# Activation slots of 8704 instead of 8320 bytes in a two-layer encoder trunk on one core

## Chip, cores and metric

The kernel runs on one core of one Trainium2 chip. The metric is the device time in microseconds of one execution. "Faster", "same" and "slower" refer to the median of the kernel before, 1147.99 us.

## What is computed

Two layers of an encoder trunk for 256 tokens of 1024 channels, float32. Each has a token mixer of three branches and a squared-ReLU MLP, both between norms that a vector c modulates:

```
h = rms_norm(x, g_pre_mix) * (1.0 + sc_m) + sh_m
proj = h @ w_in                                  # 1024 x 12296, all branches and gates
y_ret = silu(rg) * head_norm(retention(rope(rq), rope(rk), rv))
y_lru = gelu(ly) * rg_lru(causal_conv(lx, ...), ...)
y_fox = forgetting_attention(fq, fk, fv, log_sigmoid(ff + b_f))
merged = g0 * (y_ret @ ret_w_o) + g1 * (y_lru @ lru_w_o) + g2 * (y_fox @ fox_w_o)
x = x + gt_m * rms_norm(merged @ w_out, g_post_mix)
h = rms_norm(x, g_pre_mlp) * (1.0 + sc_f) + sh_f
x = x + gt_f * rms_norm(square(relu(h @ w1)) @ w2, g_post_mlp)
```

The shift, scale and gate vectors (sh, sc, gt) come from silu(c) @ ada_w + ada_b.

## The kernel before

**Products in three parts.** Every float32 operand x of a product is split into a high part xh (x rounded to the type fp32r) and a low part xl = x - xh. A product is the sum of three matmuls, xh with wh, xl with wh and xh with wl; the helper mm3 (lines 343, 344 and 345) issues the three, and all large products go through it. So a matmul reads one operand that is loaded into TensorE (an instruction of its own, on the row PEld of the profile) and one that streams through it. In the profile's rows a matmul is written out<-streamed,loaded.

**Tiling.** Weights come in chunks, each in two halves of 512 KB (128 partitions x 1024 floats). In `gemm` a weight chunk is loaded 128 columns at a time and the activations stream, 256 tokens wide: 8 k-steps x 2 column blocks x 3 = 48 matmuls of 256 columns. In `gemm_n` it is the other way round (the fv columns). In `gemm_wide` (the weights rv of layer 1, w_o, the first quarter of w1, and w2) activations are loaded and weights stream 512 columns wide. In `first_rows`, at the start of layer 0, rv and rq/rk are computed while the adaLN rows of the first norm are still being summed.

**Order and staging.** One list, ORDER, fixes the order of all weight chunks, adaLN chunks among them. A chunk's halves arrive by DMA from the SyncE queue in a ring of five raw tiles (wraw). ScalarE copies a half to the high part (whi, line 219) and VectorE subtracts (wlo, line 220); both go into rings of four slots. `prefetch` keeps two or three chunks split ahead. An adaLN chunk is not split, VectorE sums it (line 275). Smaller work (heads of retention, the gates of the recurrence, the heads of attention) is cut into steps that are put between the chunks by a budget.

**The activation slots.** The pool `up` holds, behind a first tile of 64 bytes ("phase"), twelve slots of one size: T6, T7, hh, hl, T1, T2, T3, T4, T5, T8, T9 and T10, in the order of their first use. `U(tag, ...)` returns a view of a slot; with other=True it starts 64 bytes (PHASE = 16 floats) into the slot. What lies in them: hh and hl are the high and low part of the normed input; T1 and T2 hold rq (both parts in T1), rk (T2, other=True), yr (high in T1, low in T2), fq, mh/ml and the MLP's hidden mih/mil in turn; T3 and T4 rv, yl, fv and mih/mil; T5 and T6 fk (other=True); T7 and T8 yf. Some weight chunks are split into free activation slots (wown, always with other=True; both parts of a half in one slot, 4096 bytes apart).

The pools in order are cpool (constants, pth and ptl, the modulation), wp (five wraw, four whi, four wlo, 4224 bytes each), up, tp (temporaries of 2048 bytes, uh and ul among them) and sp (small columns). A tile's place within 512 bytes follows from the sizes of what stands before it. Where `up` begins, its first slot, T6, is called place 320 in this text; wp's slots then stand at 0, 128, 256 and 384, and pth and ptl at 384.

The functions that the change touches:

Of the kernel before, what the change touches and what calls it, by code (L numbers as in the profile page):

```python
# [15 lines left out]
PSUM = bass.MemoryType.PSUM  # L16
KH = 4
PHASE = 16
NRAW = 5
NHL = 4  # L20
PL = None
# [11 lines left out]
P = 128  # L33
D = 1024
# [83 lines left out]
def trunk_kernel(ctx, tc, x, c, vec, con, ffw, wts, out):  # L118
# [4 lines left out]
    up = ctx.enter_context(tc.tile_pool(name="up", bufs=1))  # L123
# [7 lines left out]
    V, A, T = nc.vector, nc.scalar, nc.tensor  # L131
    up.tile([P, PHASE], F32, name="phase")

# [67 lines left out]
    def raw_half(i, extra=None):  # L201
        n = C if extra is None else C + NH_F
        t = wp.tile([P, KH, n], F32, name="wraw", tag="wraw", bufs=NRAW)
        src = wts[pos[0], i]
# [27 lines left out]
    def split_of(l, name, cix):  # L232
        parts = []
        for i in range(2):
            t = early.pop(0) if early else raw_half(i, ffw[l] if (name, cix) == ('fv', 0) else None)
            n = t.shape[-1]
            if (name, cix) in SLOTS:
                own = SLOTS[name, cix][i]
            elif name in ('w1', 'w2') and (name, cix) < ('w2', 12):
                own = SPARE_SLOTS[spare[0] % len(SPARE_SLOTS)]  # L240
                spare[0] += 1
            else:
                own = PL
            if own:
                both = U(own, [P, 2, KH, C], F32R, "wown", True)
                hi, lo = both[:, 0], both[:, 1]
            else:
                hi, lo = split_tiles(n)
            split(t, hi, lo)
            parts.append((hi, lo))  # L250
        pos[0] += 1
        if wide(name, cix):
            parts = [[p.rearrange("p (k j) c -> p k (j c)", k=2) for p in hl] for hl in parts]
            return [(parts[k // 2][0][:, k % 2, :], parts[k // 2][1][:, k % 2, :]) for k in range(KH)]
        return [(parts[k // KH][0][:, k % KH, :], parts[k // KH][1][:, k % KH, :]) for k in range(KD)]
# [146 lines left out]
    def U(tag, shape, dt, name, other=False):  # L402

        o, n = PHASE * other, math.prod(shape[1:])
        t = up.tile([P, 2 * D + 2 * PHASE], dt, name=name, tag=tag)[:, o:o + n]
        dims = {c: k for c, k in zip("abc", shape[1:])}
        return t.rearrange(f"p ({' '.join(dims)}) -> p {' '.join(dims)}", **dims)

# [8 lines left out]
    def new_h():  # L417
        return (U("hh", [P, KD, S], F32R, "hh"), U("hl", [P, KD, S], F32R, "hl"))
# [13 lines left out]
    def first_rows():  # L432


        silu_rows()
        xn = U("T6", [P, 2, D], F32, "xn")
        xr = U("T7", [P, KD, S], F32, "xr")

# [753 lines left out]
```

## Time and profile before

| | us |
|---|---|
| median of 3 runs | 1147.99 (1147.07 to 1148.08) |
| the profiled execution | 1149.36 |
| its span, first to last instruction | 1147.6 |
| TensorE matmul busy | 1122.1 |
| TensorE weight load busy | 1055.2 |
| VectorE busy | 872.4 |
| ScalarE busy | 616.6 |
| GpSimd busy | 33.2 |

The granted TensorE clock is 0.997 on average. The DMA moved 255 MB. A busy time is the time that is covered by an engine's records. [...] In the rows of groups the number after x is the count, then come busy us and the mean ns of one record, and behind the second bar the engine's idle time before them.

### The profile page before, as it was taken

What the parts mean: (1) busy time and instruction counts of PE and PEld (TensorE: products, weight loads), DVE (VectorE), ACT (ScalarE), POOL (GpSimd) and SP (SyncE); (2) the same over time, 40 slices, a digit from 0 to 9 for tenths busy, and PEclk for the clock granted to TensorE, in tenths of its full rate; (3) what the DMA queues carried; (4) which work ended last, traced back from release to release, by engine and by line L of the source; (5) the groups of instructions that cost most, each with busy time, mean ns of one, the idle gap of its engine ahead of it and who ended that gap; (6) DMA issues with size and microseconds to landing.
All of it is one profiled execution on the core that took longest, in us unless ns stands there. A gap on an engine that the chain in (4) does not pass through costs nothing.

```text
span 1147.6 us, 20486 instructions
## 1 busy us (share of the span) xinstructions
PE 1122.1 (98%) x8164; PEld 1055.2 (92%) x8164; DVE 872.4 (76%) x1323; ACT 616.6 (54%) x912; POOL 33.2 (3%) x54
## 2 busy tenths in 40 slices
PE   6999999999899999999999999999999999999997
PEld 5999999999899889989879999999999997989986
DVE  6898788878797789888586768877878778956543
ACT  6676594544455555444455658655444655644441
POOL 0001000000000100000020010000000001000000
PEclk9999999999999999999999999999999999999999
DMA  9954546579776569888745454565777574875541
GB/s 357 401 173 159 185 135 211 182 247 318 271 256 220 201 215 319 317 308 311 255 149 180 149 186 164 166 202 186 234 267 258 188 266 147 291 240 187 189 151 63
DMA packets 74284, 255.43 MB, mean 223 GB/s; under 512 B 10108, under 2 KB 12492, under 8 KB 74188
## 3 DMA queue, kind: packets, MB, share of 16 engines
q1 hardware_dynamic: 74188, 254.12, 65.4%
q8 instruction: 64, 1.05, 0.4%
q14 instruction: 32, 0.26, 0.1%
HBM read 253.00 MB, written 1.09 MB: 221 GB/s over the span
## 4 chain that ended last, share of the span: by engine, by line
PE 83%; DMA 6%; DVE 5%; issue 4%; ACT 1%; POOL 1%; DVEq 0%; POOLq 0%; SPq 0%; ACTq 0%
PE ps L345 24%; PE ps L343 24%; PE ps L344 24%; DMA wraw<-in_wts_dram 5%; DVE wlo L220 2%; DVE wraw L275 1%; PE xT L427 1%; PE rvp L344 1%; PE rvp L345 1%; PE rvp L343 1%; PE qkp L344 1%; PE qkp L345 1%; PE qkp L343 1%; POOL rs_v L188 1%; ACT whi L219 0%
## 5 line engine op out<-in xcount | busy, mean ns | idle before, releaser
L219 ACT CAST whi<-wraw 128x1024 fp32r<-128x1024 f32 (+1 forms) x286 | 299.2, 1050 | 282.6 <-PE ps L344 164.5
L220 DVE TENSOR_TENSOR wlo<-wraw,whi 128x1024 fp32r<-128x1024 f32 (+1 forms) x286 | 348.4, 1223 | 101.7 <-ACT whi L219 101.3
L343 PE MATMUL ps<-hh,whi 128*128 128x256 f32 x1312 | 369.5, 282 | 2.8 <-DVE fkl L650 1.2
L345 PE MATMUL ps<-hh,wlo 128*128 128x256 f32 x1312 | 368.7, 281 | 0.0
L344 PE MATMUL ps<-hl,whi 128*128 128x256 f32 x1312 | 368.3, 281 | 0.0
L343 PEld LDWEIGHTS ps<-hh,whi 128*128 128x128 f32 x1312 | 246.3, 188 | 4.3 <-PE ps L345 2.0
L345 PEld LDWEIGHTS ps<-hh,wlo 128*128 128x128 f32 x1312 | 247.7, 189 | 0.0
L344 PEld LDWEIGHTS ps<-hl,whi 128*128 128x128 f32 x1312 | 247.1, 188 | 0.2
L275 DVE SCALAR_TENSOR_TENSOR wraw<-wraw,sir 128x1024 f32<-128x1024 f32 x82 | 100.2, 1223 | 41.4 <-DMA wraw<-in_wts_dram 41.0
L220 DVE TENSOR_TENSOR wown<-wraw,wown 128x1024 fp32r<-128x1024 f32 x72 | 87.2, 1222 | 26.5 <-ACT wown L219 26.5
L219 ACT CAST wown<-wraw 128x1024 fp32r<-128x1024 f32 x72 | 74.8, 1048 | 51.8 <-PE ps L345 27.2
L345 PE MATMUL ps<-whi,mil 128*128 128x512 f32 x144 | 56.9, 395 | 0.0
L344 PE MATMUL ps<-wlo,mih 128*128 128x512 f32 x144 | 56.8, 394 | 0.0
L343 PE MATMUL ps<-whi,mih 128*128 128x512 f32 x144 | 56.7, 394 | 0.0
L344 PE MATMUL ps<-wlo,hh 128*128 128x256 f32 (+1 forms) x144 | 45.8, 318 | 0.0
L343 PE MATMUL ps<-whi,hh 128*128 128x256 f32 (+1 forms) x144 | 45.7, 317 | 0.0
L345 PE MATMUL ps<-whi,hl 128*128 128x256 f32 (+1 forms) x144 | 45.6, 317 | 0.0
L344 PE MATMUL ps<-hl,wown 128*128 128x256 f32 x160 | 45.0, 281 | 0.0
L345 PE MATMUL ps<-hh,wown 128*128 128x256 f32 x160 | 44.9, 281 | 0.0
L343 PE MATMUL ps<-hh,wown 128*128 128x256 f32 x160 | 44.8, 280 | 0.0
L343 PE MATMUL ps<-wown,mih 128*128 128x512 f32 x112 | 44.2, 395 | 0.0
L345 PE MATMUL ps<-wown,mil 128*128 128x512 f32 x112 | 44.1, 394 | 0.0
(336 smaller groups left out, 2290.2 us busy)
## 6 DMA issues: line engine op xcount, KB each, us to landing
wraw<-in_wts_dram SPq DMA_DIRECT2D x440, 512.0 KB, 4.2
wfirst<-in_wts_dram SPq DMA_DIRECT2D x28, 512.0 KB, 10.2
rows<-drow SPq DMA_DIRECT2D x10, 512.0 KB, 5.1
xs<-in_x_dram SPq DMA_DIRECT2D x2, 512.0 KB
out_dram<-xs SPq DMA_DIRECT2D x4, 256.0 KB, 2.0
csb<-in_con_dram SPq DMA_DIRECT2D x1, 768.0 KB
csb<-in_con_dram SPq DMA_DIRECT2D x1, 256.0 KB, 9.5
vsb<-in_vec_dram SPq DMA_DIRECT2D x1, 152.0 KB
```

The costliest lines, as they stand in the source:

```text
L188: eng.tensor_scalar(v, total, scale, EPS, ALU.mult, ALU.add)
L219: A.copy(hi, t)
L220: V.tensor_tensor(lo, t, hi.bitcast(F32), ALU.subtract)
L275: V.scalar_tensor_tensor(t, t, 0.5, sir, ALU.mult, ALU.mult, accum_out=m)
L343: T.matmul(ps, ah, bh, start=start, stop=False, **kw)
L344: T.matmul(ps, ah, bl, start=False, stop=False, **kw)
L345: T.matmul(ps, al, bh, start=False, stop=stop, **kw)
L427: i = T.transpose(pt[:, k, :], x[:, (k0 + k) * P:(k0 + k + 1) * P], ident)
```

## The change

The length of a slot goes from 2 x 1024 + 2 x 16 = 2080 floats (8320 bytes) to 2 x 1024 + 128 = 2176 floats (8704 bytes). Views into a slot start where they did, at its beginning or 64 bytes on. 8320 is 16 x 512 + 128, 8704 is 17 x 512. Nothing else is touched.

```
 PHASE = 16
+SLOT_PAD = 128
 NRAW = 5
...
     def U(tag, shape, dt, name, other=False):

         o, n = PHASE * other, math.prod(shape[1:])
-        t = up.tile([P, 2 * D + 2 * PHASE], dt, name=name, tag=tag)[:, o:o + n]
+        t = up.tile([P, 2 * D + SLOT_PAD], dt, name=name, tag=tag)[:, o:o + n]
         dims = {c: k for c, k in zip("abc", shape[1:])}
```

More of the change, by code (lines that the diff above doesn't have):

```diff
@@ L18 @@
 PHASE = 16
+SLOT_PAD = 128
 NRAW = 5
@@ L404, in U @@
         o, n = PHASE * other, math.prod(shape[1:])
-        t = up.tile([P, 2 * D + 2 * PHASE], dt, name=name, tag=tag)[:, o:o + n]
+        t = up.tile([P, 2 * D + SLOT_PAD], dt, name=name, tag=tag)[:, o:o + n]
         dims = {c: k for c, k in zip("abc", shape[1:])}
```

## The prediction

> **What bounds the kernel now.** I read the page first, for the shares and the chain, then TensorE's groups kept apart by shape, then the granted clock and counts in stretches, and last the timeline of single matmuls.
>
> ```profile
> span 1147.6 us, 20486 instructions
> PE 1122.1 (98%) x8164; PEld 1055.2 (92%) x8164; DVE 872.4 (76%) x1323; ACT 616.6 (54%) x912; POOL 33.2 (3%) x54
> ...
> GB/s 357 401 173 159 185 135 211 182 247 318 271 256 220 201 215 319 317 308 311 255 149 180 149 186 164 166 202 186 234 267 258 188 266 147 291 240 187 189 151 63
> ...
> PE 83%; DMA 6%; DVE 5%; issue 4%; ACT 1%; POOL 1%; DVEq 0%; POOLq 0%; SPq 0%; ACTq 0%
> ```
>
> TensorE is busy for 98% of the span and holds 83% of the chain that ended last. So the time is the number of matmuls times the step from one to the next, and the question is whether the change moves that step. A busy time is no step, because the records overlap; the step comes from counts in a stretch, or from starts in the timeline.
>
> ```profile
> core 0: us, PE busy (x), PEclk, DMA share, GB/s
> 353.00:373.00 20.00, 20.00 (x179) 1.00 0.80 263
> 724.00:809.00 85.00, 85.00 (x724) 1.00 0.58 186
> 242.00:315.00 73.00, 69.06 (x575) 1.00 0.86 294
> 816.00:878.00 62.00, 61.00 (x514) 1.00 0.78 262
> 408.00:578.00 170.00, 170.00 (x1030) 1.00 0.84 290
> 560.00:577.00 17.00, 17.00 (x75) 1.00 0.72 248
> ```
>
> The first two stretches hold matmuls of 256 columns alone, and TensorE never idles in them. A record of 0.28 us lies across each border, so about 2.4 are counted too many. 724 to 809: 85,000 / (724 - 2.4) = 117.8 ns a step. 353 to 373: 20,000 / (179 - 2.4) = 113.3 ns. Same shape, same line of code, same clock (1.00), and the faster stretch has the busier DMA (0.80 against 0.58), so neither the clock nor traffic makes the difference.
>
> What differs is which tiles are read:
>
> ```profile
> L343 PE MATMUL ps<-hh,whi 128*128 128x256 f32 x1312 | 369.5, 282 | 2.8 <-DVE fkl L650 1.2 <-DVE fvl L650 0.8 <-DVE fql L886 0.7
> L345 PE MATMUL ps<-hh,wlo 128*128 128x256 f32 x1312 | 368.7, 281 | 0.0
> L344 PE MATMUL ps<-hl,whi 128*128 128x256 f32 x1312 | 368.3, 281 | 0.0
> L344 PE MATMUL ps<-hl,wown 128*128 128x256 f32 x160 | 45.0, 281 | 0.0
> L345 PE MATMUL ps<-yrh,wlo 128*128 128x256 f32 x128 | 36.0, 281 | 0.0
> L345 PE MATMUL ps<-ylh,wlo 128*128 128x256 f32 x128 | 36.0, 281 | 0.0
> L345 PE MATMUL ps<-yfh,wlo 128*128 128x256 f32 x128 | 35.4, 276 | 0.0
> L344 PE MATMUL ps<-yfl,whi 128*128 128x256 f32 x128 | 35.4, 276 | 0.0
> ```
>
> After "<-" stands first the operand that streams, then the one that was loaded. Only the pair yfh, yfl shows 276 ns; hh/hl, yrh/yrl and ylh/yll show 280 to 282. Stretch 353 to 373 is the w_f stage, with yfh and yfl. Adding up the slots in the order in which they are first used (T6, T7, hh, hl, T1, T2, T3, T4, T5, T8, T9, T10; a slot is 8320 bytes, 16 x 512 + 128), and calling the place of T6 within 512 bytes 320, I get T7 448, hh 64, hl 192, T1 320, T2 448, T3 64, T4 192, T5 320, T8 448, T9 64, T10 192. The pairs hh/hl, yr (T1, T2) and yl (T3, T4) each lie 128 bytes apart; yf (T7, T8) is the one pair that starts at one place, and the one that is fast.
>
> **What a single stretch shows.** Rows of the timeline (start, duration, line, tiles):
>
> ```profile
> 143.71 0.28 PE L344 MATMUL lg<-ul,wown 128*128 128x256 f32 x1
> 144.95 0.28 PE L343 MATMUL ps<-hh,whi 128*128 128x256 f32 x1
> 145.06 0.28 PE L344 MATMUL ps<-hl,whi 128*128 128x256 f32 x1
> 145.42 0.28 PE L344 MATMUL ps<-hl,whi 128*128 128x256 f32 x1
> ```
>
> ```profile
> 622.96 0.28 PE L343 MATMUL rs<-rq,rk 128*128 128x256 f32 x1
> 623.30 0.28 PE L343 MATMUL ps<-hh,whi 128*128 128x256 f32 x1
> 623.89 0.28 PE L345 MATMUL ps<-hh,wlo 128*128 128x256 f32 x1
> ```
>
> uh and ul start at one place (slots of 2048 bytes, 4 x 512, in the pool behind T10, so at 192 + 128 = 320), and so do the halves of rq (T1, 320). The first burst takes 1.24 us for 11 steps, 113 ns each; as soon as hh and hl alternate, three steps take 0.36 us, 120 each. The second: three steps in 0.34 us (113), then five in 0.59 us (118). So a stream at one place can run at 113, and the jump by 128 bytes between hh and hl ends it. But equal places do not suffice:
>
> ```profile
> 136.51 0.28 PE L343 MATMUL lg<-uh,wown 128*128 128x256 f32 x1
> 137.93 0.28 PE L343 MATMUL ps<-hh,whi 128*128 128x256 f32 x1
> ...
> 80.69 0.28 PE L343 MATMUL rs<-rq,rk 128*128 128x256 f32 x1
> 81.75 0.28 PE L343 MATMUL ps<-hh,whi 128*128 128x256 f32 x1
> ...
> 351.26 0.28 PE L344 MATMUL fo<-ptl,fvh 128*128 128x256 f32 x1
> 352.57 0.28 PE L343 MATMUL ps<-yfh,whi 128*128 128x256 f32 x1
> 352.91 0.28 PE L343 MATMUL ps<-yfh,whi 128*128 128x256 f32 x1
> ```
>
> Another burst of the same kinds keeps the slow step: lg 1.42 us for 12 (118), rs 1.06 us for 9 (118), fo 1.31 us for 11 (119; pth and ptl, too, share a place). There are two paces, and a stream at one place keeps the one it fell into for a dozen matmuls. Behind the slow fo, yf was at 113 at once (0.34 us for three) and stayed there, while its weights rotated through four slots of 4224 bytes, 8 x 512 + 128, so 128 apart.
>
> **The change part by part.** The program does not change: the same instructions, queues and waits. Only addresses move. A slot of 8704 bytes is 17 x 512, so all twelve begin at 320 (those taken with other=True at 384, as T1, T5 and T6 do now). The pools behind move by 12 x 384 = 4608 = 9 x 512 bytes and keep their places; wp and cpool, in front, do not move.
>
> (1) Matmuls of 256 columns whose streamed pair comes to one place. hh/hl: 1312 x 3 from the rows, 480 with weights in own slots (160 x 3) and 192 for rq and rk in first_rows (8 x 8 x 3 by its loops): 4608. yr and yl: 128 x 3 each, 768. Together 5376, each worth up to 117.8 - 113.3 = 4.5 ns, or 24.2 us. But the gain counts only where TensorE sets the pace. In the stretches 242 to 315 and 816 to 878 it idles 3.9 and 1.0 us, and what is late there is the weights:
>
> ```profile
> 250.92 4.82 DMA wraw<-in_wts_dram
> 255.80 1.11 issue
> ...
> L344 PE MATMUL ps<-hl,whi 128*128 128x256 f32 x112 | 31.5, 281 | 0.0
> ```
>
> The first two are rows of the chain: a load of 4.8 us and its consumer's turn, one such pair behind the other. The last one is the group of hl and whi in the stretch 242 to 315, and 816 to 878 has the same: 112 x 3 x 2 = 672 of the 5376 lie there, and faster ones would only wait longer. I take nothing for them (between 0 and 672 x 4.5 = 3.0 us). That leaves 4704 x 4.5 = 21.2 us. How many get the fast pace? At worst none (the slow lg, rs and fo), at best all (yf). The streams concerned are long, 48 matmuls and more in a row, which is nearer to yf than to bursts of 12; but each is broken by small bursts that stream from 384, and after such a break it must find the fast pace again. I take 85%: 18 us.
>
> (2) Matmuls of 512 columns:
>
> ```profile
> L343 PE MATMUL ps<-whi,mih 128*128 128x512 f32 x144 | 56.7, 394 | 0.0
> L343 PE MATMUL ps<-wown,mih 128*128 128x512 f32 x112 | 44.2, 395 | 0.0
> ```
>
> (144 + 112) x 3 = 768 with mih/mil, and 96 for each of six quads (4 chunks x 4 k x 2 halves x 3: w_o and the first w1 in both layers, rv once by first_quad and once in first_rows), 1344 in all. They stream weights whose two halves share a place already; it is the loaded hh/hl, mh/ml or mih/mil that come together. Stretch 560 to 577: 17,000 / (75 - 1.7) = 231.9 ns; twice 113.3 is 226.6. So between nothing and 1344 x 5.3 = 7.1 us. No row shows such a stream with both pairs together, and streamed pairs that agree do not give it the fast pace now: I take nothing.
>
> (3) Supply. In 408 to 578 the DMA moves 290 GB/s while TensorE never idles; its 1030 matmuls in 170 us make some 600 of 256 columns and 430 of 512, so the gain there is 600 x 4.5 = 2.7 us, 1.6%, and asks for 295 GB/s. Slices of 28.7 us on the page reached 308 to 319, so I take no loss; were the supply at its end, the 2.7 us would be lost.
>
> (4) VectorE and ScalarE read the moved slots too:
>
> ```profile
> L220 DVE TENSOR_TENSOR wlo<-wraw,whi 128x1024 fp32r<-128x1024 f32 (+1 forms) x286 | 348.4, 1223 | 101.7 <-ACT whi L219 101.3
> L220 DVE TENSOR_TENSOR wown<-wraw,wown 128x1024 fp32r<-128x1024 f32 x72 | 87.2, 1222 | 26.5 <-ACT wown L219 26.5
> ```
>
> 1223 ns in the pool of weights, 1222 in the slots: nothing.
>
> Sum: -18 us. The profiled execution took 1149.36 us around its span of 1147.6, 1.37 above the median of the runs, 1147.99; I take the difference to the median: 1130 us, a gain of 1.6%.
>
> [...]
>
> **The rivals.** *Nothing happens* (1146 to 1150). Addresses are not the cause, or the common place 320 leaves the streams at the slow pace. For it: lg, rs and fo at 118 to 119 with equal places, two of them at 320; yf, the one long fast stream, stands at 448. Against it: lg and rs at 320 also ran at 113, and yf reached 113 straight from a slow burst. Then 0 x 4.5, 1148 us. The slow pace at 320 has 10 in 100, addresses that never matter 2. [...]
>
> *Only part of it* (1139 to 1146). Each break throws the stream back, and it recovers late: 20 to 40% of 21.2 us, 4 to 8 us, about 1142. 12 in 100.
>
> *Slower.* The common place is on the wrong side of the two paces: at 448 yf always fell into the fast one, at 320 streams keep the slow. Then yf, 384 matmuls, loses 4.5 ns each, 1.7 us, and if the slow pace of a stream at one place is that of fo, 119 instead of 117.8, 5376 x 1.2 = 6.5 us come on top: 8 us, 1156. It decides once fewer than 30% find the fast pace (0.3 x 21.2 against 0.7 x 6.5 + 1.7). 9 in 100.
>
> **How the numbers follow.** The forecast, fast pace for most, has 67 in 100, with its own range from 1121 (all 4704, 21, and some 6 of parts 1 and 2 left at nothing) to 1139 (40% of 21). The whole range is 1121 to 1149, which takes in the two milder rivals and leaves out about 9 above and 6 below. About 0.2%, 2.3 us, is what a measurement of this kernel can tell from no change. Faster: the forecast and the part, 0.79. Same: 0.12. Slower: 0.09.
>
> **What would show it.** In the groups by shape, hh/hl, yr and yl at 276 to 277 ns instead of 281, yf unchanged; in the long stretches a step of 113 to 114 ns; the order of work unchanged; more idle time of TensorE, with the same loads of weights late, around 242 to 315. Wrong: yf at 281, or hh/hl still at 281 while the time falls; wrong in size, if the 512-column groups (394 ns now) move as well.

## The result and the profile after

The changed kernel takes 1133.23 us (median, 1132.45 to 1133.79); the kernel before, beside it, 1148.03. The ratio is 0.9872, with a 95% interval from 0.9855 to 0.9889: 14.8 us or 1.3% faster. The prediction had 1130 us, 18 us faster.

The profiled execution's span fell from 1147.6 to 1132.0 us. From the page after (first lines and the head of the chain):

```profile
span 1132.0 us, 20486 instructions
PE 1103.7 (98%) x8164; PEld 1038.6 (92%) x8164; DVE 872.0 (77%) x1323; ACT 616.8 (54%) x912; POOL 33.9 (3%) x54
...
PE 85%; DMA 5%; DVE 4%; issue 3%; ACT 1%; POOL 1%; DVEq 0%; POOLq 0%; SPq 0%; ACTq 0%
```

The counts are the same, VectorE and ScalarE are as busy as before, and TensorE alone is 18.4 us less busy. TensorE's groups by shape, after:

```profile
L344 PE MATMUL ps<-hh,whi 128*128 128x256 f32 x1312 | 366.0, 279 | 5.1 <-DVE fql L887 3.0 <-DVE fvl L651 1.4 <-DVE fkl L651 0.6
L346 PE MATMUL ps<-hh,wlo 128*128 128x256 f32 x1312 | 364.4, 278 | 0.1
L345 PE MATMUL ps<-hl,whi 128*128 128x256 f32 x1312 | 364.3, 278 | 0.0
L345 PE MATMUL ps<-hl,wown 128*128 128x256 f32 x160 | 44.3, 277 | 0.0
L346 PE MATMUL ps<-yrh,wlo 128*128 128x256 f32 x128 | 35.4, 276 | 0.0
L346 PE MATMUL ps<-ylh,wlo 128*128 128x256 f32 x128 | 35.4, 276 | 0.0
L346 PE MATMUL ps<-yfh,wlo 128*128 128x256 f32 x128 | 35.4, 277 | 0.0
```

yr and yl fell from 281 to 276 ns, as yf had been. hh and hl stand at 278 and 279, between the two paces. The idle time before the first group rose from 2.8 to 5.1 us.

The stretch from w_r to the end of w_l in layer 0, after (busy, count, clock, DMA share, GB/s):

```profile
165.00:239.00 74.00, 74.00 (x655) 1.00 0.63 202
```

74,000 / (655 - 2.4) = 113.4 ns a step. In the timeline, a stream of hh and hl after ropv:

```profile
89.28 0.28 PE L344 MATMUL ps<-hh,whi 128*128 128x256 f32 x1
...
92.10 0.28 PE L344 MATMUL ps<-hh,whi 128*128 128x256 f32 x1
...
92.57 0.28 PE L345 MATMUL ps<-hl,whi 128*128 128x256 f32 x1
...
93.48 0.28 PE L344 MATMUL ps<-hh,whi 128*128 128x256 f32 x1
```

The first 24 steps take 2.82 us (117.5 each). At 92.10 the chunk's second half begins, which lies in another weight slot; from 92.57 on eight steps take 0.91 us (114). The next stream does not get free:

```profile
95.85 0.28 PE L345 MATMUL ps<-hl,whi 128*128 128x256 f32 x1
...
101.39 0.28 PE L344 MATMUL rs<-rq,rk 128*128 128x256 f32 x1
```

47 steps in 5.54 us, 118 each, through the change of slots as well. So both paces go on side by side. From here on "the fast share" is the share of steps of at most 115 ns between the starts of hh/hl matmuls of 256 columns, counted over the whole trace (pauses over 150 ns left out). It rose from 10% to 67%, and the mean step fell from 117.76 to 114.85 ns. For yr and yl all steps are fast (113.3); yf, fast before, went from 113.4 to 113.9 ns.

The 117.8 of before and the slow 117.8 of after look alike only in the mean. Before, with the pair apart, the steps of hh and hl vary, mostly between 115 and 122 ns, and only 2% of them are at 114 or less; the 10% are mostly single steps of 115. After, a slow stream steps evenly, mostly at 117 to 119 ns, and 65% of all steps are at 114 or less.

Counted over all streams, pauses left out, no stream after the change switches pace within a weight slot, apart from the first five steps of a stream or a slot. At a change of slots all of the more than 100 streams at 113 ns stay there. Those at 118 ns come to 113 in 29 of 43 cases where the streamed tile lay 64 bytes behind the loaded one (mod 256: both places taken within 256 bytes) and then lies 192 behind, and in none of the 3 the other way round.

Last, what became of the lead. The first matmul of fv and the first of the attention heads, before:

```profile
244.09 0.29 PE L343 MATMUL pf<-whi,hh 128*128 128x264 f32 x1
...
297.52 0.28 PE L922 MATMUL fs<-ch,sel 128*128 128x256 f32 x1
```

and after:

```profile
239.04 0.29 PE L344 MATMUL pf<-whi,hh 128*128 128x264 f32 x1
...
293.42 0.28 PE L923 MATMUL fs<-ch,sel 128*128 128x256 f32 x1
```

A lead of 5.05 us at the one is 4.10 at the other: between them the weights' DMA sets the pace (the chain after is loads of 4.6 to 5.7 us, one behind the other, and TensorE idles 2.4 of 54.4 us), and 0.95 us of what TensorE saved is spent waiting. Layer 1 gives back 1.1 us there (13.3 and 12.2).

### The profile page after: what moved, and what is told of

It is laid out like the page before. It is cut to its first block, busy times and chain, and to the rows that moved or that the text cites. A ratio compares the mean times of both kernels' runs of the same rounds, so it can differ in the third digit from the quotient of the medians.

```text
span 1132.0 us, 20486 instructions
## 1 busy us (share of the span) xinstructions
PE 1103.7 (98%) x8164; PEld 1038.6 (92%) x8164; DVE 872.0 (77%) x1323; ACT 616.8 (54%) x912; POOL 33.9 (3%) x54
## 4 chain that ended last, share of the span: by engine, by line
PE 85%; DMA 5%; DVE 4%; issue 3%; ACT 1%; POOL 1%; DVEq 0%; POOLq 0%; SPq 0%; ACTq 0%
PE ps L346 25%; PE ps L344 25%; PE ps L345 25%; DMA wraw<-in_wts_dram 5%; DVE wlo L221 2%; PE xT L428 1%; DVE wraw L276 1%; PE rvp L345 1%; PE rvp L346 1%; PE rvp L344 1%; PE qkp L344 1%; PE qkp L345 1%; PE qkp L346 1%; POOL rs_v L189 1%; ACT whi L220 0%
## 5 line engine op out<-in xcount | busy, mean ns | idle before, releaser
L346 PE MATMUL ps<-hh,wlo 128*128 128x256 f32 x1312 | 364.4, 278 | 0.1
L345 PE MATMUL ps<-hl,whi 128*128 128x256 f32 x1312 | 364.3, 278 | 0.0
```

The lines of the kernel that those rows point to most:

```text
L345: T.matmul(ps, ah, bl, start=False, stop=False, **kw)
L346: T.matmul(ps, al, bh, start=False, stop=stop, **kw)
```

## The experiments

The theory: a matmul's step depends on where in 256 or 512 bytes its two streams begin; a jump between the high and low part of the streamed operand throws it to the slow pace. The first rival: it is the slots' length or their common place that counts, not the pair.

**e1_low128: the pairs apart again, in the long slots.**

```
-        o, n = PHASE * other, math.prod(shape[1:])
+        o, n = PHASE * other + 32 * (tag in ('hl', 'T2', 'T4', 'T8')), math.prod(shape[1:])
```

> Slots of 8704 bytes as in the change, but what lies in hl, T2, T4 and T8 (the low parts) begins 128 bytes further on, so every high and low part is 128 bytes apart again. If the distance within a streamed pair sets the step, hh/hl, yr, yl and now yf too run at 280 to 282 ns a record, a step of 117.5 to 118, and the time is 1147 to 1150 us. If it is the length of the slots, or the place of the high parts, the time stays at 1133 us.

1149.07 us, ratio 1.0004 (0.9994 to 1.0015): the whole gain is gone. (Two small changes cancel in this: yf at 117.8 instead of 113.4 ns costs 1.7 us against the kernel before, and the 512-column matmuls at 230.5 instead of 231.6 save 1.5.) Groups of this kernel:

```profile
L345 PE MATMUL ps<-hl,whi 128*128 128x256 f32 x1312 | 368.1, 281 | 0.0
L346 PE MATMUL ps<-yrh,wlo 128*128 128x256 f32 x128 | 36.0, 281 | 0.0
L346 PE MATMUL ps<-yfh,wlo 128*128 128x256 f32 x128 | 35.9, 281 | 0.0
```

yf, fast in both kernels, is slow here. The length of the slots is ruled out.

**e2_low256: 256 bytes apart.** The same line with 64 floats instead of 32.

> As e1_low128, but the low parts begin 256 bytes further on. If what repeats in the memory repeats every 256 bytes, 256 apart is as good as nothing apart and the time is 1133 us within 4; if it repeats every 512, it is 1147 to 1150 us.

1131.47 us, ratio 0.9852 (0.9828 to 0.9875), fast share 65%: as the change. So 256 bytes apart did as well as one place, where 128 apart lost the whole gain (1149.07 us in e1_low128); "the same place within 512" asks for more than these runs needed.

**e11_low64: 64 bytes apart.** The same line with 16 floats.

> e1_low128 with 64 instead of 128 bytes between high and low part. If any distance that is no multiple of 256 throws a stream back, hh/hl, yr and yl run at 117 to 118 a step and the time is 1146 to 1150 us; if small distances do less, between 1136 and 1145.

1152.96 us, ratio 1.0048 (1.0033 to 1.0063), fast share 14% (single steps of 115 ns; 1% are at 114 or less), mean step of hh/hl 118.7 ns. That is slower than the kernel before, which I had not expected. 64 bytes on, the low part lies 128 behind half of the weight slots and level with the other half; in this trace hh/hl, yr, yl and yf step at 117.7 ns on the first half and at 119.5 on the second. Level was worse than apart in e8_rel0 too (120.2 ns, below).

**e4_hh_only: one pair alone.** The kernel before, with one slot longer:

```
-        t = up.tile([P, 2 * D + 2 * PHASE], dt, name=name, tag=tag)[:, o:o + n]
+        t = up.tile([P, 2 * D + 2 * PHASE + 96 * (tag == 'hh')], dt, name=name, tag=tag)[:, o:o + n]
```

> The kernel before, with the slot of hh alone 384 bytes longer: hh and hl begin at one place, and yr, yl and also T7 and T8 (yf) lie 128 apart. If the pair decides, hh/hl fall to 277 to 279 ns as in the change, yr and yl stay at 281 and yf rises from 276 to 281; gain about 13 us at hh/hl less 1.7 at yf, 1136 to 1139 us. If it is the common length of all slots, yf stays at 276 and the time at 1148 us.

1138.93 us, ratio 0.9915 (0.9895 to 0.9935). Its groups:

```profile
L344 PE MATMUL ps<-hl,whi 128*128 128x256 f32 x1312 | 364.5, 278 | 0.0
L345 PE MATMUL ps<-yrh,wlo 128*128 128x256 f32 x128 | 36.0, 281 | 0.0
L344 PE MATMUL ps<-yfl,whi 128*128 128x256 f32 x128 | 35.9, 281 | 0.0
```

Each pair by itself: hh/hl fast as in the change, yr still slow, yf now slow. Here the profile of one kernel holds the effect in both directions.

**e3_at448: the common place moved by 128 bytes.**

```
-    up.tile([P, PHASE], F32, name="phase")
+    up.tile([P, PHASE + 32], F32, name="phase")
```

> The change, with the first tile of the pool 192 instead of 64 bytes long, so that all slots (and the pools behind) begin at 448 instead of 320. In the profile after the change a stream that is slow never turned fast inside a weight slot, only where the weights change slots, and only from a slot that lies 64 bytes before the activations (mod 256) to one that lies 192 before; every chunk begins at 64. If only the distance within the pair matters, 1133 us within 2, with about two thirds of the hh/hl matmuls at 113. If the place against the weights decides how a stream begins, chunks now begin at 192: more than 85% at 113, and 1126 to 1129 us.

1131.28 us, ratio 0.9853 (0.9827 to 0.9879); fast share 77%, less than the 85% expected, and the ratio's interval overlaps that of the change. Of the 13 streams that follow a float32 product or transpose and begin at the chunks' usual place, 12 now begin fast; in the change 1 of 13 does. Streams at 118 ns now come to 113 where 64 becomes 192 from slot to slot, which lies at the chunks' borders here. I took this for proof that the place against the weights decides how a stream begins, and built on it.

**e5_rel192, e6_rel64, e8_rel0: the weights at one place.** All ring slots of whi and wlo begin at one place (mod 256), so a stream sees no jump between ring slots. The three differ in the pool's first tile alone (48, 16 and 64 floats).

```
-        return (wp.tile([P, KH, n], F32R, name="whi", tag="whi", bufs=NHL),
-                wp.tile([P, KH, n], F32R, name="wlo", tag="wlo", bufs=NHL))
+        return [wp.tile([P, 1088], F32R, name=tag, tag=tag, bufs=NHL)[:, :KH * n].rearrange("p (k c) -> p k c", k=KH)
+                for tag in ("whi", "wlo")]
...
-SLOT_PAD = 128
+SLOT_PAD = 64
```

> Slots of 8448 bytes (33 x 256), whi and wlo slots of 4352 (17 x 256), and the pool 128 bytes further on: now every streamed activation lies 192 bytes behind every loaded weight (mod 256), through all slots. Theory: the place of streamed against loaded decides how a stream begins after a break; at 192 nearly all begin fast and none is thrown back, so 85 to 97% of the hh/hl matmuls at 113 and 1125 to 1129 us; only the streams behind ropv and fo (pth stays where it is) begin slow and, without a change of place to free them, stay slow. Rival: only the jump of the weight slots frees a stream, and without it less than 60% are fast, 1135 us or more.

1140.88 us, ratio 0.9934 (0.9912 to 0.9957), fast share 32%: the theory of the beginning fell, its rival came true.

> As e5_rel192, but the pool stays where it was, so that every streamed activation lies 64 bytes behind every weight of the rings (192 behind those in own slots). Theory: at 64 streams begin slow and never turn; fast only what comes in from an already fast stream (those behind lg or w1's own-slot weights): 20 to 45% of hh/hl fast, 1136 to 1143 us. Rival, only the distance within the pair counts: as the change, 1131 to 1134 us.

1143.03 us, ratio 0.996 (0.9944 to 0.9976), fast share 24%. As expected in size, but it is hardly worse than 192 and so does not speak for the reason given.

> As e5_rel192, but activations and ring weights begin at one and the same place (0 behind; 192 behind the own-slot weights). If only the distance within the streamed pair counts, 1131 to 1134 us. If the place against the weights counts, this is the meeting of both streams at one place and should be the worst: hardly any of the hh/hl with ring weights at 113, 1140 us or more.

1156.0 us, ratio 1.0081 (1.0058 to 1.0104), slower than the kernel before. The stretch of w_r to w_l, in this kernel:

```profile
170.00:240.00 70.00, 70.00 (x585) 1.00 0.60 192
```

70,000 / (585 - 2.4) = 120.2 ns: with both streams beginning at one place even a pair without a jump ran slower here than the slow pace of 117.8. These are activations that stream past ring weights. For the 512-column matmuls of the same kernel, where weights stream past loaded activations, one place cost nothing: 228.4 ns a step there, 230.2 where the weights lie 64 behind.

**e7_all_pairs: every stream at one place against every weight.** e5_rel192 with fq, fv and rv at other=True, fk without it, and pth/ptl 64 bytes further on.

> e5_rel192 with the rest brought to the same two places: fq, fv and rv (loaded) begin 64 bytes into their slots, fk (streamed) at the slot's beginning, pth and ptl (streamed) 64 bytes further on. So everything that streams 256 columns of activations lies at 192 behind everything that is loaded. Theory: no break is left, over 97% of all 256-column matmuls fast, 1122 to 1126 us. Rival: breaks come from switching between kinds of matmul and not from places, then it is as e5_rel192 within 1 us.

1138.77 us, ratio 0.993 (0.9906 to 0.9953), fast share 42%: the theory's 97% and 1126 us did not come. The rival was nearer: the time is 2.1 us below that of e5_rel192, and the intervals overlap. The shortest account of what goes on is in two stretches of this one kernel, the same code at the same places in layer 0 and in layer 1:

```profile
165.00:240.00 75.00, 75.00 (x665) 1.00 0.61 198
721.00:799.00 78.00, 78.00 (x665) 1.00 0.56 184
```

75,000 / 662.6 = 113.2 ns and 78,000 / 662.6 = 117.7. In layer 1 a stream had fallen into the slow pace earlier, and it stayed in it from the start of w_r to the end of w_l. Nothing is to be seen that would free it: no slot begins elsewhere, and TensorE never pauses. Over the whole traces it is the same: of streams that had been slow for more than eight matmuls, none turned fast at a change of weight slots that brought no jump, 0 of 122 in e5_rel192, 0 of 106 in e6_rel64 and 0 of 95 here. So it is at the jumps of the weight slots, to which the theory had given no part, that slow streams came free (29 of 43 in the profile after the change), and there the jumps hurt none of the more than 100 fast ones. (Not every jump does it: the only five from 64 to 192 that met a slow stream in e6_rel64, from a ring slot into an activation slot, freed none.)

**e9_jumps and e10_jumps448: more such jumps.** Ring slots begin at one place, but within them each k-step lies 128 bytes further on:

```
-    def split_tiles(n):
+    def split_tiles(n, jump=False):
+        w = 288 if jump else n
+        return [wp.tile([P, 1152], F32R, name=tag, tag=tag, bufs=NHL)[:, :KH * w].rearrange(
+            "p (k c) -> p k c", k=KH)[:, :, :n] for tag in ("whi", "wlo")]
...
-                hi, lo = split_tiles(n)
+                hi, lo = split_tiles(n, n == C and not wide(name, cix))
```

with SLOT_PAD = 64; e10_jumps448 also has the pool's first tile at 48 floats.

> The runs at fixed places showed slow streams that stayed slow for 100 us and more: nothing frees a stream but a jump of the loaded weights. Here the ring slots of the weights are 4608 bytes and begin at one place, but inside a slot each k-step lies 128 bytes further on (rows of 288 instead of 256 floats; chunks read 512 wide stay as they were); activation slots of 8448, pool where the change has it (64 behind the weights at the first k-step, then 192, 64, 192). So the jump from 64 to 192 comes twice in a slot instead of once in two. Theory: a slow stream is freed after some 12 to 24 matmuls, 75 to 90% of hh/hl fast, 1127 to 1131 us. Rival, the place at which a stream begins decides alone: as the change or slower, 1133 us or more.

1130.36 us, ratio 0.985 (0.9834 to 0.9867), fast share 86%, as the theory had it. Of the streams that had been slow for more than eight matmuls, 18 of 18 turned fast at a jump from 64 to 192 and 0 of 16 at one from 192 to 64. The time alone would not tell this version from the change (after_again, below, on the same chip: 0.9848 to 0.9883). By the steps, hh/hl save 3.9 us more than in the change (114.0 against 114.85 ns), and the 512-column matmuls cost 1.7 us more (231.4 against 230.1 ns).

> e9_jumps with the pool 128 bytes further on: streams begin 192 behind the weights, and the weights that stream 512 wide lie 64 behind the loaded activations, the pairing that took 229 ns a step instead of 232 in the change. Theory: 80 to 95% of hh/hl fast and all 512-column matmuls at about 229: 1124 to 1129 us. Rival as before: e3_at448's 1131 us or more.

1127.47 us, ratio 0.9826 (0.9811 to 0.984), fast share 92%. Its groups and the stretch of w_r to w_l:

```profile
L346 PE MATMUL ps<-hl,whi 128*128 128x256 f32 x1312 | 362.6, 276 | 0.0
L345 PE MATMUL ps<-whi,mih 128*128 128x512 f32 x144 | 56.1, 389 | 0.0
```

```profile
162.00:236.00 74.00, 74.00 (x655) 1.00 0.62 197
```

hh and hl are at 276 now, and the 512-column group, 394 in the kernel before and 393 in the change, is at 389 (a mean step of 228.9 ns). The stretch steps at 74,000 / 652.6 = 113.4 ns, as in the change, where it was fast already. This version beats both kernels, as expected.

**after_again: the change once more,** on the chip of the last three and beside them.

> The change itself, on the chip of the three others: every theory has it at 1132 to 1135 us with two thirds of the hh/hl matmuls at 113; it tells how much of a difference to the others is the chip's.

1132.23 us, ratio 0.9865 (0.9848 to 0.9883), fast share 66%. The interval of e10_jumps448 lies wholly below it, so the 4.8 us between the two are no matter of the chip.

## Why the prediction was right, and where its size was off

- **The mechanism** was right: the change moves addresses alone, and the step of matmuls whose streamed pair comes together falls (hh/hl from 117.76 to 114.85 ns, yr and yl from 117.8 to 113.3). e1_low128 takes the pairs apart again and leaves the slots long, and nothing is left of the gain. Of the signs named, 276 to 277 ns came for yr and yl; hh and hl stopped at 278 and 279, and the 512-column matmuls moved too, which was the sign of a wrong size.
- **Part 1, mis-sized.** "I take 85%: 18 us" for 4704 matmuls. Measured from starts: hh/hl 2.9 ns on 4608, 13.4 us; yr and yl 4.45 on 768, 3.4 us: 16.8 us, at a fast share of 67% and 100%. Without the 672 (2.9 ns each, 1.95 us) that is 14.9 us in place of 18. The 85% failed for hh/hl: I saw that breaks throw a stream back and that it must find the fast pace again, but not that it does so only where the weights jump from 64 to 192, and in 14 of 43 cases not even there. yf, from which I took the share, is broken only once in a layer, near its beginning.
- **The 672 matmuls in the DMA's stretches** counted nothing in the sum, and that held: their share of the 16.8 us is what TensorE waits more (0.95 and 1.1 us given back between fv and the heads). All pauses over 300 ns between two matmul starts, less a step of 0.23 us each, grew from 19.1 to 22.1 us, 3.0 us; the other 1 us of it is spread over the span.
- **Part 2, taken at nothing,** brought 2.0 us: the mean step of 512 columns fell from 231.64 to 230.13, on 1316 counted. It is not evenly spread. After the change the step is 229.3 where the streamed weights lie 64 behind the loaded activation and 231.9 where they lie 192 behind. Before, the high and low part of one product lay one at 64 and one at 192; now both lie at the same, and two thirds of these matmuls at 64.
- **Parts 3 and 4** held: TensorE has no new pause in the MLP stages (busy 166.0 of 166 us and 162.0 of 162, DMA at 295 and 195 GB/s), VectorE's busy time is 872.0 after 872.4.
- **The sum:** 16.8 + 2.0 less 3.0 of new waits is 15.8; the span fell by 15.6 and the median by 14.8. Luck helped the number: part 1 was 3.1 us too high, and part 2's 2.0 us, taken at nothing, made up for two thirds of that.
- **The rivals.** "Nothing happens" rested on slow bursts at 320, and rightly held that a common place does not suffice; it lost because long streams meet jumps at which they came free (29 of 43). "Slower" was right that streams at 320 mostly begin slow (12 of 13 behind a float32 product or transpose) and wrong that they stay so, and yf lost 0.5 ns a step instead of 4.5; but its kind exists: e8_rel0 and e11_low64 are slower than the kernel before (1156.0 and 1152.96 us). That addresses never matter is refuted by e1_low128, and by e6_rel64 and e8_rel0, which differ only in where the pool of activations begins, 64 bytes behind the weights or level with them, and take 1143.03 and 1156.0 us.

**What stays open.** Why the place of one stream against the other moves the step, and why slow streams come free at a jump from 64 to 192, was not measured; the runs show that they often do (29 of 43 in the change, 18 of 18 in e9_jumps), and that at the jump back they do not (0 of 3 and 0 of 16). How a stream begins after a break is not settled either: behind a float32 product or transpose 12 of 13 began fast at 192 in e3_at448, and in e5_rel192 and e7_all_pairs, at 192 too, 4 of 14.

## What to carry to other kernels

Where TensorE sets the pace and its matmuls come in pairs or triples that stream related tiles, let these begin at the same place within 256 bytes: here 0 and 256 bytes apart took 1133.23 and 1131.47 us, 64 and 128 apart 1152.96 and 1149.07. Activations that streamed 256 columns wide past weights at that same place were the slowest of all here (120.2 ns in e8_rel0), weights that streamed 512 wide past activations were not (228.4 ns, against 230.1 in the change), so try the place against the loaded operand for each shape. Read the step from start times or counts, not from the mean of the records, and look for two values (113 and 118 ns here): a mixture says that the stream has two paces, and then the question is what puts it into the longer step and what gets it out. A run of 12 matmuls was too short to tell: in the kernel before, one burst of lg stepped at 113 ns and another at 118.

## What the runs showed of the hardware that was not expected

Two matmul streams of the same code at the same addresses ran at 113.2 ns a step for 75 us on end in layer 0 and at 117.7 for 78 us in layer 1 (e7_all_pairs); the slow one had been slow before. Fixed relations between the streams were not the best ones here: with all weights at one place the gain shrank to 0.7% (e5_rel192) or became a loss of 0.8% (e8_rel0), while weights that jump by 128 bytes at each k-step brought 1.7% (e10_jumps448). And the place that was worst for one shape was not so for another: level with the loaded operand, 256 columns took 120.2 ns a step, the longest of all runs, and 512 columns 228.4, shorter than the change's 230.1 (e8_rel0).
